# One decoder layer on one core: value banks emptied bank by bank, a pair's queries and keys projected one step ahead, the last product of the stick-breaking weights on VectorE

## The chip, the core and the metric

The kernel runs on one core of a Trainium2 chip. It is one launch, and the metric is the device time of that launch in microseconds. The engines that matter are TensorE (PE: matrix products, written into the eight banks of PSUM), VectorE (DVE), ScalarE (ACT), GpSimd (POOL) and the queue of SyncE (SP), which issues the loads of the weights.

## What is computed

One post-norm decoder layer over 512 positions of width 1024, batch 1:

```python
u = x * (1.0 + sc1) + sh1                       # adaLN, from c @ w_ada + b_ada
proj = u @ w_in                                 # q,k,v of both branches, forget logits, two gates
y_fox = forgetting_attention(q_a, k_a, v_a)     # 8 heads of 64: softmax(q k / 8 + c_t - c_s), causal
y_sb  = stick_breaking_attention(q_b, k_b, v_b) # 8 heads: beta[t,s] * prod_(s<j<t) (1 - beta[t,j])
merged = sigmoid(g_a) * (y_fox @ w_fox_proj) + sigmoid(g_b) * (y_sb @ w_sb_proj)
x = layer_norm(alpha * x + (1 + gt1) * (merged @ w_o))
u2 = x * (1.0 + sc2) + sh2
h_gate, h_val = split(causal_depthwise_conv(u2 @ w_up))
x = layer_norm(alpha * x + (1 + gt2) * ((silu(h_gate) * h_val) @ w_down))
```

In the stick-breaking branch beta is sigmoid(q k / 8). The product over the later keys is a running product of 1 - beta from the right; the weight is beta times that product.

## The kernel before

**Stages.** First comes an accumulation over the eight input tiles into all eight PSUM banks (lines 261 to 274): queries of pair 0 and 1, keys of pair 0, the values of the stick-breaking branch for the four blocks of 128 positions (banks `grp[3]` to `grp[6]`), and the forget logits. Then come sixteen heads of attention, eight stick-breaking and eight forgetting, in pairs (lines 727 to 762). Behind them come the branch projections, the output projection with the first norm, the up-projection and the down-projection.

**Every large product is made of three** (`mm3`, line 109): a float32 operand is split into a high part, written by ScalarE (`hi_of`, line 75), and a low part, written by VectorE (`lo_of`, line 78, input minus high part). A bank of PSUM that is emptied this way is read by ScalarE first and by VectorE after it, and an eight-bank pool (`bank`, line 66) hands the bank on when both have read it.

**A head** has three stages on TensorE. `stage_a` (line 411) makes the scores into three banks, four blocks of query positions in all; the one with 512 keys has the bank b == 1 to itself. For a stick-breaking head ScalarE then writes 1 - beta (`om`, line 452) and beta (`pt`, line 453) of each bank, VectorE scans `om` (line 456, four scans of 127, 383, 255 and 511 keys), and GpSimd multiplies `pt` by the scanned `om` (line 457, four products of the same sizes). `stage_b` (line 467) transposes the weights into three banks, which ScalarE and VectorE split into `ph`/`pl` and `ptc`. `stage_c` (line 490) multiplies by the values (`vv`).

**Fillers.** Projections that later heads and stages need stand in a list, `stream`: per pair the queries and the keys, then gates, value projections of the other branch and branch projections. A projection is a generator that gives three products at a time. `fill(n)` (line 710) takes n products from the list; `fill_to(mark)` (line 723) takes products until the list has passed a mark. `marks[(p, "k")]` is the place behind the keys of pair p. These fillers stand between the stages of the heads, so that TensorE has work while the other engines turn scores into weights. In the loop over the heads (lines 743 to 761) step n makes `stage_a` of head n + 2, `stage_b` of head n + 1 and `stage_c` of head n, with fillers between; `fill_to` for the pair of head n + 2 stands right ahead of that `stage_a`.

**What sets the order.** The order on SyncE is that of the code. On the other engines a scheduler sets it when the program is built, from the order of the code, the dependencies and the buffers that are free; the engines then run their instructions strictly in that order. So a change of the code can move instructions that it does not name.

## Time and profile before

| | us |
|---|---|
| runs before | 772.07, 772.87, 773.32 (median 772.87) |
| profiled execution, its own time | 772.12 |
| profiled execution, span of the core | 770.3 |
| TensorE busy in the span | 748.1 |
| VectorE busy | 549.4 |
| ScalarE busy | 350.4 |
| GpSimd busy | 185.7 |

The profile is one execution. Times in it run from the start of the span; 1.8 us of the execution's time lie outside of it. A row of the timeline gives the start, the duration, the engine, the line, the operation, what it writes and reads, how many like it follow each other, and in brackets how long the engine stood idle ahead of it and what ended that. Names of buffers are without their numbers there. Durations of instructions that follow each other overlap, so the distance from start to start is what an instruction costs in a row of them.

### The profile page before, as it was taken

How to read it: one execution, taken by the hardware profiler on the slowest of the kernel's cores; microseconds unless marked ns; L12 is line 12 of the kernel's file. 1: busy time of each engine (PE TensorE's matmuls, PEld its weight loads, DVE VectorE, ACT ScalarE, POOL GpSimd, SP SyncE). 2: the span in 40 equal slices, each digit the busy share in tenths (PEclk: the TensorE clock that was granted, in tenths of full speed). 3: DMA queues.
4: the chain of work that ended last, by engine and by line, in shares of the span. 5: the costliest groups of instructions: out<-in, count | busy, mean ns of one | idle time of the engine just before them, and what ended most of it. 6: DMA issues, size and time to landing. Idle time of an engine off the chain costs nothing.

```text
span 770.3 us, 9560 instructions
## 1 busy us (share of the span) xinstructions
PE 748.1 (97%) x3556; PEld 620.6 (81%) x3556; DVE 549.4 (71%) x822; ACT 350.4 (45%) x583; POOL 185.7 (24%) x138
## 2 busy tenths in 40 slices
PE   5998999999999999999999999999999999999995
PEld 3886887788888888888889888888888888888885
DVE  6979889966687977776676787686656665533666
ACT  3357686717667556333145434444444433222400
POOL 1025424510000011364000780000000043945500
PEclk9999999999999999999999999999999999999998
DMA  8951253542333323455302524354332214323202
GB/s 310 403 204 55 83 165 131 175 161 83 110 110 110 127 93 136 144 190 164 137 1 73 201 79 145 118 177 137 114 105 93 100 55 165 120 98 127 65 28 83
DMA packets 31105, 99.68 MB, mean 129 GB/s; under 512 B 4273, under 2 KB 4785, under 8 KB 31058
## 3 DMA queue, kind: packets, MB, share of 16 engines
q1 hardware_dynamic: 30546, 99.00, 37.0%
q8 instruction: 28, 0.46, 0.2%
q14 instruction: 19, 0.16, 0.1%
q0 software_dynamic: 512, 0.07, 0.1%
HBM read 96.88 MB, written 2.10 MB: 128 GB/s over the span
## 4 chain that ended last, share of the span: by engine, by line
PE 86%; DVE 6%; ACT 5%; DMA 1%; issue 1%; SPq 0%; DVEq 0%; ACTq 0%
PE ps L110 17%; PE ps L111 17%; PE ps L112 17%; PE ps L941 5%; PE ps L940 5%; PE ps L942 5%; PE ps L254 4%; PE ps L495 2%; PE ps L821 2%; PE ps L820 2%; PE ps L819 2%; PE ps L477 2%; DVE om L456 1%; DMA wa<-in_wa 1%; ACT wh L75 1%
## 5 line engine op out<-in xcount | busy, mean ns | idle before, releaser
L78 DVE TENSOR_TENSOR wl<-raw,wh 128x1024 fp32r<-128x1024 f32 (+2 forms) x106 | 143.8, 1357 | 101.0 <-ACT wh L75 100.5
L75 ACT ACTIVATE wh<-raw 128x1024 fp32r<-128x1024 f32 (+2 forms) x106 | 110.4, 1042 | 108.1 <-PE ps L942 39.9
L110 PE MATMUL ps<-u2h,wh 128*128 128x512 f32 (+1 forms) x376 | 141.4, 376 | 0.0
L111 PE MATMUL ps<-u2l,wh 128*128 128x512 f32 (+1 forms) x376 | 141.2, 376 | 0.0
L112 PE MATMUL ps<-u2h,wl 128*128 128x512 f32 (+1 forms) x376 | 141.2, 375 | 0.0
L587 POOL TENSOR_TENSOR raw<-raw,gt 128x1024 f32<-128x1024 f32 x22 | 60.7, 2774 | 187.1 <-DVE gt L550 157.6
L110 PE MATMUL ps<-uh,wh 128*128 128x512 f32 x232 | 92.9, 400 | 2.2 <-DVE vv L78 2.2
L112 PE MATMUL ps<-uh,wl 128*128 128x512 f32 x232 | 90.8, 391 | 0.0
L111 PE MATMUL ps<-ul,wh 128*128 128x512 f32 x232 | 90.8, 391 | 0.0
L110 PEld LDWEIGHTS ps<-u2h,wh 128*128 128x128 f32 x376 | 70.8, 188 | 12.9
L111 PEld LDWEIGHTS ps<-u2l,wh 128*128 128x128 f32 x376 | 70.8, 188 | 12.8
L112 PEld LDWEIGHTS ps<-u2h,wl 128*128 128x128 f32 x376 | 70.8, 188 | 12.6
L110 PEld LDWEIGHTS ps<-uh,wh 128*128 128x128 f32 x232 | 43.6, 188 | 10.7 <-DVE vv L78 2.5
L112 PEld LDWEIGHTS ps<-uh,wl 128*128 128x128 f32 x232 | 43.6, 188 | 9.4
L111 PEld LDWEIGHTS ps<-ul,wh 128*128 128x128 f32 x232 | 43.7, 188 | 7.9
L940 PE MATMUL ps<-wh,hh 128*128 128x512 f32 x128 | 49.8, 389 | 0.0
L941 PE MATMUL ps<-wl,hh 128*128 128x512 f32 x128 | 49.8, 389 | 0.0
L942 PE MATMUL ps<-wh,hl 128*128 128x512 f32 x128 | 49.8, 389 | 0.0
L457 POOL TENSOR_TENSOR pt<-pt,om 128x127 f32<-128x127 f32 (+3 forms) x32 | 40.0, 1278 | 33.8 <-DVE om L456 28.7
L75 ACT ACTIVATE hh<-cv 128x512 fp32r<-128x512 f32 x22 | 13.9, 631 | 59.6 <-DVE cv L920 59.6
L575 POOL TENSOR_TENSOR raw<-raw,gt 128x1024 f32<-128x1024 f32 x8 | 21.1, 2645 | 78.0 <-DVE m L78 42.2
L919 ACT ACTIVATE cv<-cv 128x512 f32<-128x512 f32 x22 | 13.9, 632 | 54.5 <-DVE cv L914 54.5
(188 smaller groups left out, 1463.0 us busy)
## 6 DMA issues: line engine op xcount, KB each, us to landing
raw<-in_wup SPq DMA_DIRECT2D x44, 512.0 KB, 3.3
raw<-in_wa SPq DMA_DIRECT2D x32, 512.0 KB, 3.3
raw<-in_wct SPq DMA_DIRECT2D x29, 512.0 KB, 3.2
raw<-in_wdn SPq DMA_DIRECT2D x22, 512.0 KB, 3.2
wa<-in_wa SPq DMA_DIRECT2D x14, 512.0 KB, 8.7
raw<-in_wp SPq DMA_DIRECT2D x8, 512.0 KB, 3.3
raw<-in_wo SPq DMA_DIRECT2D x8, 512.0 KB, 3.6
raw<-in_w SPq DMA_DIRECT2D x7, 452.0 KB, 8.3
```

What stands on the lines that cost most here:

```text
L75: S.activation(o, i, AF.Copy, scale=scale)
L78: return V.tensor_tensor(o, i, fl(hi), ALU.subtract)
L110: PE.matmul(ps, wh, ah, start=first, stop=False)
L111: PE.matmul(ps, wh, al, start=False, stop=False)
L112: PE.matmul(ps, wl, ah, start=False, stop=last)
L254: PE.matmul(grp[g], w, u, start=j == 0 and n == 0, stop=j == KT - 1 and n == (1 if g == 7 else 2))
L457: G.tensor_tensor(pt[b][:, s : e - 1], pt[b][:, s : e - 1], om[:, s + 1 : e], ALU.mult)
L575: G.tensor_tensor(r, r, gt[0], ALU.mult)
L587: G.tensor_tensor(r, r, gt[1], ALU.mult)
L940: PE.matmul(ps, hh[j][:, tb], w[0], start=first, stop=False)
L941: PE.matmul(ps, hh[j][:, tb], w[1], start=False, stop=False)
L942: PE.matmul(ps, hl[j][:, tb], w[0], start=False, stop=last)
```

## The change

It has three parts. The four value banks are emptied bank by bank (both halves of a bank, then the next bank) where they were emptied half by half (the first half of all banks, then the second). The fourth product of a stick-breaking head, that of bank b == 1 with 511 keys, goes from GpSimd to VectorE. And `fill_to` for a pair's keys moves: for pairs 2, 3, 4, 6 and 7 it now stands ahead of `stage_c` of the step before, where it stood ahead of `stage_a`; for pairs 1 and 5 it stays.

```diff
--- before.py
+++ after.py
@@ -454,7 +454,7 @@
                 for s, e in SEG[b]:
                     d0 = om[:, s + 1 : e][:, ::-1]
                     V.tensor_tensor_scan(d0, d0, zer.broadcast_to([P, e - s - 1]), 1.0, ALU.mult, ALU.add)
-                    G.tensor_tensor(pt[b][:, s : e - 1], pt[b][:, s : e - 1], om[:, s + 1 : e], ALU.mult)
+                    (V if b == 1 else G).tensor_tensor(pt[b][:, s : e - 1], pt[b][:, s : e - 1], om[:, s + 1 : e], ALU.mult)
         d["pt"] = pt
         scored.add(idx(br, h))
         if br == 0 and h + 4 < NH:
@@ -731,10 +731,11 @@
     q_evac(1, 1, grp[2])
     fill(6)
     stage_a(1, 0)
-    for half in range(2):
-        for j in range(NB):
+    for j in range(NB):
+        for half in range(2):
             v_evac(1, j, half, grp[3 + j])
-        fill(6)
+        if j % 2 == 1:
+            fill(6)
     stage_a(1, 1)
     fill(12)
     stage_b(1, 0)
@@ -745,7 +746,7 @@
             forget(last)
         f1, f2, f3 = FILL[n // 8]
         if n + 2 < 16:
-            if n % 2 == 0:
+            if n in (0, 8):
                 fill_to(marks[(n // 2 + 1, "k")])
             last = hd[heads[n + 1]].get("last")
             stage_a(*heads[n + 2])
@@ -753,6 +754,8 @@
         if n + 1 < 16:
             stage_b(*heads[n + 1])
         fill(f2)
+        if n % 2 == 1 and n != 7 and n + 3 < 16:
+            fill_to(marks[((n + 3) // 2, "k")])
         stage_c(b, h)
         if n == 7:
             lim[0] = marks["y0"]
```

What becomes of it on the engines is told by the order of the built program. Three places are shown, before and after.

**VectorE at the value banks.** `om_100` and `pt_96` belong to bank b == 1 of the first head; `vv_101` to `vv_108` are the eight halves of the value banks `ps_4` to `ps_7`; `wl_123` is the low half of a weight tile for a filler. Before:

```order
L78 TENSOR_TENSOR vv_101_617<-ps_4_106,vv_101_617 128x2x128
L78 TENSOR_TENSOR vv_102_620<-ps_5_107,vv_102_620 128x2x128
L78 TENSOR_TENSOR vv_103_623<-ps_6_108,vv_103_623 128x2x128
L78 TENSOR_TENSOR vv_104_626<-ps_7_109,vv_104_626 128x2x128
L78 TENSOR_TENSOR vv_105_635<-ps_4_106,vv_105_635 128x2x128
L78 TENSOR_TENSOR vv_106_638<-ps_5_107,vv_106_638 128x2x128
L78 TENSOR_TENSOR wl_123_706<-raw_85_562,wh_122_705 128x1024
L78 TENSOR_TENSOR vv_107_641<-ps_6_108,vv_107_641 128x2x128
L78 TENSOR_TENSOR vv_108_644<-ps_7_109,vv_108_644 128x2x128
```

After:

```order
L457 TENSOR_TENSOR pt_96_598<-pt_96_598,om_100_612 128x511
L78 TENSOR_TENSOR vv_101_617<-ps_4_106,vv_101_617 128x2x128
L78 TENSOR_TENSOR wl_123_706<-raw_85_562,wh_122_705 128x1024
L78 TENSOR_TENSOR vv_102_620<-ps_4_106,vv_102_620 128x2x128
L78 TENSOR_TENSOR vv_103_623<-ps_5_107,vv_103_623 128x2x128
L78 TENSOR_TENSOR vv_104_626<-ps_5_107,vv_104_626 128x2x128
L78 TENSOR_TENSOR vv_105_635<-ps_6_108,vv_105_635 128x2x128
L78 TENSOR_TENSOR vv_106_638<-ps_6_108,vv_106_638 128x2x128
L78 TENSOR_TENSOR vv_107_641<-ps_7_109,vv_107_641 128x2x128
L78 TENSOR_TENSOR vv_108_644<-ps_7_109,vv_108_644 128x2x128
```

The product stands ahead of all eight halves; the weight tile `wl_123` has moved from behind the sixth half to behind the first one; and the two halves of bank `ps_4` are now the first and the third row of their kind, where they were the first and the fifth. Further on in the same queue another weight tile, `wl_151`, has moved from behind the transposed weights of the second head to ahead of the second half of the keys of pair 1 (`m2_3`).

**TensorE at the third head.** `ps_120` is the bank of the filler (a gate), `ps_132` the last bank of the third head's scores, `ps_140`, `ps_143` and `ps_146` those of the second head's transposes, `ps_148` the bank of the next filler. Before:

```order
L425 MATMUL ps_132_739<-mskb_96,identb_88 128x128
L110 MATMUL ps_120_702<-uh_59_374,wh_88_568 128x512
L111 MATMUL ps_120_702<-ul_60_375,wh_88_568 128x512
L112 MATMUL ps_120_702<-uh_59_374,wl_89_569 128x512
L110 MATMUL ps_120_702<-uh_67_420,wh_88_568 128x512
L111 MATMUL ps_120_702<-ul_68_421,wh_88_568 128x512
L112 MATMUL ps_120_702<-uh_67_420,wl_89_569 128x512
L477 MATMUL ps_140_788<-ident_77,pt_112_668 128x128
L477 MATMUL ps_140_788<-ident_77,pt_114_670 128x128
L477 MATMUL ps_140_788<-ident_77,pt_112_668 128x128
L477 MATMUL ps_140_788<-ident_77,pt_113_669 128x128
L477 MATMUL ps_143_797<-ident_77,pt_114_670 128x128
```

After:

```order
L425 MATMUL ps_132_739<-mskb_96,identb_88 128x128
L477 MATMUL ps_140_788<-ident_77,pt_112_668 128x128
L477 MATMUL ps_140_788<-ident_77,pt_114_670 128x128
L477 MATMUL ps_140_788<-ident_77,pt_112_668 128x128
L477 MATMUL ps_140_788<-ident_77,pt_113_669 128x128
L477 MATMUL ps_143_797<-ident_77,pt_114_670 128x128
L477 MATMUL ps_143_797<-ident_77,pt_112_668 128x128
L477 MATMUL ps_143_797<-ident_77,pt_113_669 128x128
L477 MATMUL ps_146_805<-ident_77,pt_113_669 128x128
L477 MATMUL ps_146_805<-ident_77,pt_112_668 128x128
L477 MATMUL ps_146_805<-ident_77,pt_113_669 128x128
L110 MATMUL ps_148_816<-uh_19_149,wh_90_572 128x512
```

Before, the scores of the third head stood in the middle of the filler `ps_120`, and six of its products lay between them and the transposes. After, the whole filler stands ahead of the scores (some of it between the three groups of transposes of the first head), and scores, transposes of the second head and the next filler follow each other directly.

**TensorE at the first forgetting head.** `ps_340` before and `ps_336` after are the same bank by use: the keys of pair 4. `ps_354` holds that head's scores. `ps_350` before and `ps_346` after are the next filler. Before:

```order
L112 MATMUL ps_340_1733<-uh_71_458,wl_337_1698 128x512
L110 MATMUL ps_350_1782<-uh_19_149,wh_343_1740 128x512
L111 MATMUL ps_350_1782<-ul_20_150,wh_343_1740 128x512
L112 MATMUL ps_350_1782<-uh_19_149,wl_344_1741 128x512
L110 MATMUL ps_350_1782<-uh_27_190,wh_343_1740 128x512
L111 MATMUL ps_350_1782<-ul_28_191,wh_343_1740 128x512
L112 MATMUL ps_350_1782<-uh_27_190,wl_344_1741 128x512
L110 MATMUL ps_350_1782<-uh_35_236,wh_343_1740 128x512
L111 MATMUL ps_350_1782<-ul_36_237,wh_343_1740 128x512
L112 MATMUL ps_350_1782<-uh_35_236,wl_344_1741 128x512
L420 MATMUL ps_354_1794<-m1_345_1768,s1_338_1725 128x256
```

After:

```order
L112 MATMUL ps_336_1717<-uh_71_458,wl_333_1682 128x512
L110 MATMUL ps_346_1766<-uh_19_149,wh_339_1724 128x512
L111 MATMUL ps_346_1766<-ul_20_150,wh_339_1724 128x512
L112 MATMUL ps_346_1766<-uh_19_149,wl_340_1725 128x512
L495 MATMUL ps_350_1778<-ph_288_1429,vv_102_620 128x512
L495 MATMUL ps_350_1778<-ph_291_1437,vv_104_626 128x384
L495 MATMUL ps_350_1778<-ptc10_504,vv_106_638 128x256
L495 MATMUL ps_350_1778<-ptc10_504,vv_108_644 128x256
L495 MATMUL ps_350_1778<-pl_289_1430,vv_102_620 128x512
L495 MATMUL ps_350_1778<-pl_292_1438,vv_104_626 128x384
L495 MATMUL ps_350_1778<-ptc11_505,vv_106_638 128x256
L495 MATMUL ps_350_1778<-ptc11_505,vv_108_644 128x256
```

Before, nine products of the filler stand between the last one of the keys and the first scores that read them. After, three of them, the eight products of `stage_c` of the sixth head and another fifteen of the filler stand there. The first heads of pairs 6 and 7 are changed alike: nine before; after, fifteen and a `stage_c`. At pairs 2 and 3 the keys already stood well ahead of the scores that read them, and the order of TensorE there is the same before and after, apart from buffer numbers and two fillers that move within the transposes of the sixth head. ScalarE's program has two more loads of its function table (16 for 14), which the scheduler placed among the forgetting heads.

## Prediction

> **What bounds the kernel now.** I read the page first: its busy shares and its chain.
>
> ```profile
> PE 748.1 (97%) x3556; PEld 620.6 (81%) x3556; DVE 549.4 (71%) x822; ACT 350.4 (45%) x583; POOL 185.7 (24%) x138
> PE 86%; DVE 6%; ACT 5%; DMA 1%; issue 1%; SPq 0%; DVEq 0%; ACTq 0%
> ```
>
> TensorE is busy for 97% of the span and carries 86% of the chain that ended last. The change neither adds nor removes a product of TensorE, so all that it can move are the times in which TensorE waits. The waits of TensorE, summed by who ended them, come next; those in the attention stage are these:
>
> ```profile
> PE ps L110 <- DVE vv L78: 2.2, 1, 2.2
> PE ps L421 <- DVE m L78: 1.8, 2, 1.1
> PE ps L477 <- DVE yf L502: 1.0, 1, 1.0
> PE ps L420 <- ACT m L75: 0.4, 2, 0.2
> ```
>
> VectorE ends nearly all of them. The windows of the timeline say why: in one such stretch VectorE has 23.4 of 25 us filled.
>
> ```profile
> 120.00:145.00 25.00, 23.11 (x117) 18.59 (x115) 23.42 (x31) 17.84 (x33) 12.27 (x15) 1.00 0.37 128
> ```
>
> The fourth column group is VectorE's. So the question is what the change does to VectorE's queue at the few places where TensorE waits for it. Behind the attention stage TensorE has no wait that the change touches; what is won or lost ahead of 310 us stays to the end.
>
> **The change, part by part: the value banks and the product of the first three heads.** The rows around the two largest waits, from the timelines of VectorE, ScalarE and TensorE:
>
> ```profile
> 64.42 2.08 DVE L78 TENSOR_TENSOR vv<-ps,vv 128x256 fp32r<-128x256 f32 x6
> 66.58 1.23 DVE L78 TENSOR_TENSOR wl<-raw,wh 128x1024 fp32r<-128x1024 f32 x1
> 67.72 0.75 DVE L78 TENSOR_TENSOR vv<-ps,vv 128x256 fp32r<-128x256 f32 x2
> 68.38 3.75 DVE L456 TENSOR_TENSOR_SCAN om<-om,zer 128x127 f32<-128x127 f32 x4
> 72.05 0.65 DVE L78 TENSOR_TENSOR m<-ps,m 64x512 fp32r<-64x512 f32 x1
> 73.97 0.69 DVE L78 TENSOR_TENSOR m<-ps,m 64x512 fp32r<-64x512 f32 x1 [0.80 <-ACT m L75]
> 74.70 1.16 DVE L78 TENSOR_TENSOR pl<-ps,ph 128x512 fp32r<-128x512 f32 x2
> ```
>
> ```profile
> 64.88 0.71 ACT L75 ACTIVATE vv<-ps 128x256 fp32r<-128x256 f32 x2 [0.92 <-DVE vv L78]
> 72.74 1.20 ACT L75 ACTIVATE m<-ps 64x512 fp32r<-64x512 f32 x2 [1.60 <-DVE m L78]
> ```
>
> ```profile
> 66.23 0.50 PE L110 MATMUL ps<-uh,wh 128*128 128x512 f32 x1 [2.22 <-DVE vv L78]
> 72.76 0.38 PE L421 MATMUL ps<-m,s 68*128 68x256 f32 x1 [1.11 <-DVE m L78]
> 73.97 0.48 PE L110 MATMUL ps<-uh,wh 128*128 128x512 f32 x1
> 77.24 0.39 PE L110 MATMUL ps<-uh,wh 128*128 128x512 f32 x1
> ```
>
> At 66.23 TensorE starts a filler in the bank whose fifth half VectorE has just read (six halves from 64.42, 0.33 apart, 0.42 each: the fifth ends at 66.16). At 72.76 it goes on with the third head's scores once the low keys (`m`, ended 72.70) are there. At 77.24 the next filler begins; this row is my yardstick, since the same work lies ahead of it before and after.
>
> What a product of 511 keys costs on VectorE the trace does not show. The nearest rows are two-input operations of 512 columns:
>
> ```profile
> 92.81 1.06 DVE L529 SCALAR_TENSOR_TENSOR ac<-raw,cTs,ac 128x512 f32<-128x512 f32 x1
> 95.43 0.74 DVE L529 SCALAR_TENSOR_TENSOR ac<-raw,cTs,ac 128x512 f32<-128x512 f32 x1
> 142.83 1.58 DVE L78 TENSOR_TENSOR wvl<-raw,wvh 128x512 fp32r<-128x512 f32 x1
> 144.80 0.68 DVE L78 TENSOR_TENSOR wvl<-raw,wvh 128x512 fp32r<-128x512 f32 x1
> 121.98 1.27 DVE L78 TENSOR_TENSOR chi<-fq,chi 8x512 fp32r<-8x512 f32 x1
> ```
>
> In a row, 144.80 costs 0.60 to the next start, which is the lower end. But the same operation took 1.06 at 92.81, right behind the last scan, against 0.74 at 95.43, and another took 1.58 against 0.68: there GpSimd was still at its products. The moved product stands in the place of the row at 92.81, with GpSimd's product of 255 keys still running, so I take 0.60 + 0.32 = 0.92 where it follows the scan directly, and 0.60 where another operation has taken that delay already. [...]
>
> Now VectorE's queue as the built order has it. The product takes 64.42 to 65.34. The first half follows at 65.34, the weight tile at 65.67; that tile costs 1.14 (66.58 to 67.72), so the second half of the first bank starts at 66.81 and ends at 67.23: the filler starts at 67.3 where it started at 66.23, 1.1 later, although its bank is third in place of fifth. The other banks now go one after the other, and within a bank the two engines take turns: ScalarE's row at 64.88 shows that the second half of a bank waits until VectorE has read the first. A bank then costs 0.42 (VectorE), 0.39 (ScalarE; two take 0.71), 0.33 to VectorE's next start, and about 0.05 of hand-over: 1.19, where eight halves in a row cost 0.33 each. The first half of the second bank starts at 67.14, that of the fourth at 69.52, and its second half ends at 70.8. The second head's scans start there, where they started at 68.38: 2.4 later. [...]
>
> From the scans to the keys VectorE took 68.38 to 72.70, 4.32. From 70.8, with another product of 0.92, that is 76.05; TensorE has its fillers done by about 74 (24 of them from 67.3, and the first head's transposes) and waits for it. The rest of the scores takes 1.21 (72.76 to 73.97) and ends at 77.3. Now the transposes follow without six fillers between. All eight banks hold something then (keys, gate, three of transposes, three of scores), so each group needs a bank that VectorE has just let go, and the filler behind them the last one. VectorE: the third bank of transposes to 76.5, the weight tile that was moved here to 77.7 (1.14 again); the second keys, for which ScalarE takes 1.20 from 76.05, to 78.35; the two `pl` 1.16, to 79.5. The yardstick row comes at 79.5 in place of 77.24: **2.3 later**. With products at 0.60 it is 1.6; with ScalarE's sigmoid 0.2 late at the second scan it is 2.5.
>
> Is this caught up? VectorE and ScalarE go on from TensorE:
>
> ```profile
> 84.03 1.06 ACT L75 ACTIVATE wh<-raw 128x1024 fp32r<-128x1024 f32 x1 [1.97 <-PE ps L111]
> 85.13 1.22 DVE L78 TENSOR_TENSOR wl<-raw,wh 128x1024 fp32r<-128x1024 f32 x1 [2.28 <-ACT wh L75]
> 100.89 0.63 ACT L75 ACTIVATE yh<-yf 128x512 fp32r<-128x512 f32 x1 [1.14 <-DVE yf L502]
> 128.75 0.38 PE L421 MATMUL ps<-m,s 68*128 68x256 f32 x1 [0.68 <-DVE m L78]
> 144.93 0.50 PE L420 MATMUL ps<-m,s 128*128 128x512 f32 x1 [0.26 <-DVE ptc L78]
> ```
>
> At 85.13 VectorE has been idle for 2.28 until a weight tile that ScalarE could split only when TensorE had used its buffer. That idle time takes in the third head's product, and from there everything shifts with TensorE. So I count no catching up.
>
> **The products of heads four to eight.** From 85.13 VectorE has no gap until it releases ScalarE at 100.89; the fourth head's product (0.60, behind the row at 92.81) comes through to there, and on through ScalarE to the sixth head's scans. The sixth head's product adds 0.92 and takes away the slow `chi` at 121.98 (1.27 against some 0.68). At 128.75 TensorE waits for VectorE, so it is later by 0.60 + 0.92 - 0.59 = 0.93 less what the new order gains by placing a weight tile of ScalarE's (1.06, as at 84.03) into a gap; half of that, 0.5, gives +0.4 (0 to 0.9). At 144.93 the seventh head's product (0.60) replaces GpSimd's, for which the row at 142.83 had waited 0.90: -0.3. Sum **+0.1** (-0.5 to +0.8).
>
> **The keys one step ahead.** Three times TensorE reached scores whose keys ScalarE had not written yet. Here are two of them (181.22 and 245.39), and between them the same kind of scores without a wait (193.42):
>
> ```profile
> 180.66 0.39 PE L112 MATMUL ps<-uh,wl 128*128 128x512 f32 x1
> 181.22 0.74 PE L420 MATMUL ps<-m,s 128*128 128x256 f32 x3 [0.18 <-ACT m L75]
> 181.80 0.39 PE L110 MATMUL ps<-uh,wh 128*128 128x512 f32 x1
> 182.48 0.28 PE L421 MATMUL ps<-m,s 68*128 68x256 f32 x1
> 183.58 0.48 PE L110 MATMUL ps<-uh,wh 128*128 128x512 f32 x1
> 193.42 0.28 PE L420 MATMUL ps<-m,s 128*128 128x256 f32 x1
> 195.01 0.48 PE L110 MATMUL ps<-uh,wh 128*128 128x512 f32 x1
> 244.90 0.39 PE L112 MATMUL ps<-yh,wl 128*128 128x512 f32 x1
> 245.39 0.73 PE L420 MATMUL ps<-m,s 128*128 128x256 f32 x3
> ```
>
> A filler lasts 0.23 from start to start, so scores could have begun at 180.89: 0.33 lost. In two pieces they took 0.58 + 1.10 = 1.68 against 1.59 in one (193.42 to 195.01): 0.09 more. At 245.39 it is 0.26 + 0.09, and I take the same for the third (pair 7). Fifteen fillers and a `stage_c` hide the splitting afterwards (nine did not), so all three go: **-1.1** (-1.2 to -0.8). At pair 5 nothing changes. What is late next: `stage_c` of the waiting head comes after the keys, its inputs long done. The price at the end, where the list of fillers runs out earlier and the last head's transposes meet its `stage_c` with only the other head's eight products between, I put at nothing (0 to 0.5), and the two table loads of ScalarE too.
>
> **The sum.** 772.12 + 2.3 + 0.1 - 1.1 = 773.4 in the profiled execution. That execution lies 0.75 under the median of 772.87, so against the median I say 774.2, 0.17% more. A measurement of this kernel can tell about 0.2% from no change, 1.5 us, so this is no change by a narrow margin; the forecast's own range, from the ends above, is 773.0 to 775.4.
>
> **Rivals.** *VectorE becomes the bound from 85 to 145 us (slower).* The five later products would cost 0.92 each, with neither `chi` nor the row at 142.83 any quicker. At 128.75 three count, 2.8; at 144.93 the fourth, 0.9. For it: 23.42 of 25 us busy. Against it: GpSimd's slowing goes with its product. It gives 2.3 + 3.7 - 1.1 = +4.9, 777.8; it decides from two products at full price on. *The delay is swallowed (faster, or nearly).* If VectorE's chain to 145 does not hang on TensorE, the 2.3 only fill TensorE's waits there (1.8 and 1.0 in the first list, in part). Then -1.1 remain, and with 0.3 from each of two unslowed `ac` about -1.7: 771.2. Against it stands the row at 84.03. *The change does nothing that counts*: early products at 0.60, +1.6 - 0.5 - 1.1 = 0: 772.9.
>
> **Chances.** Forecast 0.6, of which 0.35 under +0.2% and 0.25 over it; VectorE bound 0.17; swallowed 0.13, of which 0.12 faster; nothing 0.10. So slower 0.42, same 0.46, faster 0.12. The range from 771.5 to 776.5 leaves out the far half of both outer rivals.
>
> **What would show it.** Right: a first filler about 1 us later than 66.23, scans of the second head at 70 to 71, the row of 77.24 at 79 to 80, no ScalarE wait at the first scores of pairs 4, 6 and 7, and the product on VectorE at 0.9 to 1.1 behind a scan. Wrong: the yardstick row near 77, or waits of TensorE between 85 and 145 that together grow by more than 1 us or vanish.

## The result and the profile after

The changed kernel takes 777.58 us (median of 4 runs, 777.02 to 778.18) against 773.1 us before (4 runs, 772.07 to 773.42): ratio 1.0062, 95% interval 1.0049 to 1.0074. The forecast was 774.2, with 776.5 as the upper end. The profiled execution took 777.68 (span 775.9), 5.56 more than that of before, of which the forecast had 1.3.

The busy shares and the chain, from the page of after:

```profile
PE 752.1 (97%) x3556; PEld 624.7 (81%) x3556; DVE 557.5 (72%) x830; ACT 353.9 (46%) x585; POOL 174.2 (22%) x130
...
PE 88%; DVE 5%; ACT 4%; issue 1%; DMA 1%; SPq 0%; DVEq 0%; ACTq 0%
```

TensorE is busy for 4.0 us more, although it makes the same 3556 products; why is told below. VectorE has the eight products (830 for 822). The waits of TensorE in after, summed by who ended them; what before had stands at the start of the prediction:

```profile
PE ps L110 <- DVE vv L78: 3.3, 1, 3.3
...
PE ps L421 <- DVE m L78: 1.6, 1, 1.6
PE ps L111 <- DVE yl L78: 1.0, 1, 1.0
PE ps L477 <- DVE m L78: 0.9, 1, 0.9
PE ps L420 <- ACT m L75: 0.5, 1, 0.5
```

The wait for `vv` grew by 1.1, as forecast. The wait for `yl`, the low part of an input of the branch projections, is new, and it lies where nothing was forecast. To see how much each place cost, the start of a product of TensorE is compared with the start of the same product before, at places ahead of which the same products lie in both:

```
at (us of before)    60.1   66.2   77.2  128.7  144.9  276    320    end
later in after      +0.07  +1.16  +3.94  +5.04  +4.86  +3.73  +5.47  +5.53
added since the last       +1.09  +2.78  +1.10  -0.18  -1.13  +1.74  +0.06
```

Less the 0.07 that was there at the start: +3.87 up to the yardstick row (forecast +2.3), +0.92 over heads four to eight (+0.1), -1.13 for the keys (-1.1), +1.74 at the end of attention (0 to 0.5). VectorE around the value banks in after:

```profile
64.54 0.87 DVE L457 TENSOR_TENSOR pt<-pt,om 128x511 f32<-128x511 f32 x1
65.45 0.42 DVE L78 TENSOR_TENSOR vv<-ps,vv 128x256 fp32r<-128x256 f32 x1
65.79 1.22 DVE L78 TENSOR_TENSOR wl<-raw,wh 128x1024 fp32r<-128x1024 f32 x1
66.92 0.75 DVE L78 TENSOR_TENSOR vv<-ps,vv 128x256 fp32r<-128x256 f32 x2
68.12 0.76 DVE L78 TENSOR_TENSOR vv<-ps,vv 128x256 fp32r<-128x256 f32 x2 [0.45 <-ACT vv L75]
...
71.02 3.75 DVE L456 TENSOR_TENSOR_SCAN om<-om,zer 128x127 f32<-128x127 f32 x4
74.87 0.88 DVE L457 TENSOR_TENSOR pt<-pt,om 128x511 f32<-128x511 f32 x1
75.67 0.67 DVE L78 TENSOR_TENSOR m<-ps,m 64x512 fp32r<-64x512 f32 x1
...
77.99 1.23 DVE L78 TENSOR_TENSOR wl<-raw,wh 128x1024 fp32r<-128x1024 f32 x1 [1.19 <-ACT wh L75]
79.25 0.69 DVE L78 TENSOR_TENSOR m<-ps,m 64x512 fp32r<-64x512 f32 x1
```

Down to 75.67 this is the forecast queue: the product at 0.87 and 0.88 (forecast 0.92), a bank in 1.20 from start to start (66.92 to 68.12; forecast 1.19), the scans at 71.02 (70.8), the low keys done at 76.34 (76.05). Then comes what was not forecast: VectorE stands still for 1.19 ahead of the weight tile at 77.99, because ScalarE's half of the tile is late, and ScalarE waited for a product of TensorE. ScalarE's row and then TensorE's:

```profile
76.90 1.06 ACT L75 ACTIVATE wh<-raw 128x1024 fp32r<-128x1024 f32 x1 [1.86 <-PE ps L111]
```

```profile
67.39 0.80 PE L110 MATMUL ps<-uh,wh 128*128 128x512 f32 x1 [3.34 <-DVE vv L78]
67.98 0.63 PE L111 MATMUL ps<-ul,wh 128*128 128x512 f32 x1
...
75.04 0.40 PE L111 MATMUL ps<-ul,wh 128*128 128x512 f32 x1
...
79.99 0.55 PE L477 MATMUL ps<-ident,pt 128*128 128x128 f32 x3 [0.91 <-DVE m L78]
...
81.18 0.50 PE L110 MATMUL ps<-uh,wh 128*128 128x512 f32 x1
```

The same product of 512 columns lasts 0.63 behind the wait and 0.40 later. Set out by windows of 3.41 us (the seventh number of a row, ahead of the DMA share, is the granted clock of TensorE), after shows:

```profile
63.04:66.46 3.42, 1.01 (x5) 0.42 (x4) 3.29 (x4) 1.75 (x4) 1.83 (x2) 1.00 0.00 0
66.46:69.87 3.41, 2.48 (x6) 2.00 (x7) 2.51 (x7) 1.42 (x5) 0.00 (x0) 0.50 0.44 154
69.87:73.29 3.42, 3.42 (x13) 2.76 (x12) 2.91 (x6) 3.18 (x8) 1.71 (x2) 0.50 0.00 0
...
131.32:134.74 3.42, 1.78 (x12) 1.36 (x11) 2.38 (x5) 0.93 (x3) 1.40 (x3) 1.00 0.82 280
134.74:138.15 3.41, 3.41 (x13) 2.41 (x12) 3.06 (x6) 2.54 (x5) 1.04 (x2) 0.50 0.03 10
```

After a window in which TensorE had work for only 1.01 of 3.42 us, the clock was granted at 0.50 for two windows; after one with 1.78, for one. Before, the window around the same wait had more work, and the clock stayed:

```profile
64.91:68.33 3.42, 2.10 (x12) 1.76 (x13) 3.35 (x8) 3.42 (x9) 0.96 (x1) 1.00 0.00 0
```

In after the half clock lasts 6.83 us from 66.46 and 3.41 from 134.74, and these two starts are 68.28 apart, 20 times 3.41. The windows of before lie some 1.9 later (64.91 for 63.04), though the program is only 0.07 apart at 60 us: where they lie against the program differs between these two executions.

That counts beside the length of the wait. In the profiled execution of the kernel with the keys alone (below), whose wait at this place is 2.24, where before had 2.22 and its window 2.10 us of work, a window happened to hold only 1.73 us of work, and the clock fell to 0.50 from 66.30 to 69.71. It cost nothing at the yardstick row (+0.00): the wait for the low keys, 1.11 before, took it up. In after the two windows were more than that wait could take up, and TensorE came to the third head's scores after the low keys.

At the end of attention, the rows of VectorE, GpSimd and TensorE in after, each in its own timeline:

```profile
311.80 1.97 DVE L78 TENSOR_TENSOR yl<-yf,yh 128x512 fp32r<-128x512 f32 x1 [0.70 <-ACT yh L75]
```

```profile
310.83 2.39 POOL L575 TENSOR_TENSOR raw<-raw,gt 128x1024 f32<-128x1024 f32 x1 [14.19 <-DMA raw<-in_wo]
```

```profile
313.83 0.49 PE L111 MATMUL ps<-yl,wh 128*128 128x512 f32 x1 [1.04 <-DVE yl L78]
```

And before:

```profile
307.18 0.69 DVE L78 TENSOR_TENSOR yl<-yf,yh 128x512 fp32r<-128x512 f32 x1 [0.70 <-ACT yh L75]
```

```profile
308.84 2.50 POOL L575 TENSOR_TENSOR raw<-raw,gt 128x1024 f32<-128x1024 f32 x1 [12.76 <-DMA raw<-in_wo]
```

Before, `yl` took 0.69 and was done at 307.87, before GpSimd began the product on the output weights. After, GpSimd began first, and `yl` took 1.97 and ended 0.55 behind GpSimd's end (313.77 against 313.22). TensorE, which has few fillers left there, waits for it. This meeting is the step of 1.28 in TensorE's delay between 307 and 310 us of before. Another 0.35 of the 1.74 is at the place that the prediction had named: the last head's `stage_c` comes so close behind its transposes that it waits for ScalarE's `ph` (two products take 0.93 in place of 0.58).

### The profile page after: what moved, and what is told of

Same layout as the page of the kernel before. It is cut to its first block, busy times and chain, and to the rows that moved or that the text cites. A ratio compares the mean times of both kernels' runs of the same rounds, so it can differ in the third digit from the quotient of the medians.

```text
span 775.9 us, 9551 instructions
## 1 busy us (share of the span) xinstructions
PE 752.1 (97%) x3556; PEld 624.7 (81%) x3556; DVE 557.5 (72%) x830; ACT 353.9 (46%) x585; POOL 174.2 (22%) x130
## 4 chain that ended last, share of the span: by engine, by line
PE 88%; DVE 5%; ACT 4%; issue 1%; DMA 1%; SPq 0%; DVEq 0%; ACTq 0%
PE ps L110 17%; PE ps L111 17%; PE ps L112 17%; PE ps L254 6%; PE ps L944 5%; PE ps L945 5%; PE ps L943 5%; PE ps L824 2%; PE ps L822 2%; PE ps L823 2%; PE ps L495 2%; PE ps L477 2%; ACT wh L75 1%; DVE wl L78 1%; PE ps L420 1%
## 5 line engine op out<-in xcount | busy, mean ns | idle before, releaser
L110 PE MATMUL ps<-uh,wh 128*128 128x512 f32 x232 | 94.5, 407 | 3.3 <-DVE vv L78 3.3
L112 PEld LDWEIGHTS ps<-u2h,wl 128*128 128x128 f32 x376 | 70.8, 188 | 12.9
L111 PEld LDWEIGHTS ps<-u2l,wh 128*128 128x128 f32 x376 | 70.8, 188 | 12.8
L110 PEld LDWEIGHTS ps<-u2h,wh 128*128 128x128 f32 x376 | 70.8, 188 | 12.6
L457 POOL TENSOR_TENSOR pt<-pt,om 128x127 f32<-128x127 f32 (+2 forms) x24 | 29.0, 1234 | 41.3 <-DVE om L456 31.6
```

Source lines behind the costliest of these rows:

```text
L110: PE.matmul(ps, wh, ah, start=first, stop=False)
L111: PE.matmul(ps, wh, al, start=False, stop=False)
L112: PE.matmul(ps, wl, ah, start=False, stop=last)
L457: (V if b == 1 else G).tensor_tensor(pt[b][:, s : e - 1], pt[b][:, s : e - 1], om[:, s + 1 : e], ALU.mult)
```

## The experiments

Two questions were open. For the attention stage: **Theory A** says that a good part of the delay is the slower clock that follows TensorE's longer waits; its rival, **Theory B**, says that VectorE's queue alone makes it, whatever the clock. For the end: **Theory A** says that `yl` is caught behind GpSimd's product; the rival is that the fillers taken forward are simply missing there. The table gives, for each kernel, how much later TensorE is than before at five places, less what it was at 60 us (from one profiled execution each). The times with the experiments are medians; the kernel before stood at 772.79, 773.13, 772.96, 773.02 and 773.08 beside them.

| kernel | at 60 | 77.2 | 128.7 | 144.9 | 276 | 320 |
|---|---|---|---|---|---|---|
| changed | +0.07 | +3.87 | +4.97 | +4.79 | +3.66 | +5.40 |
| the same again | +0.26 | +3.72 | +4.86 | +4.70 | +3.59 | +7.79 |
| value banks alone | +0.62 | +1.79 | +1.96 | +1.95 | +1.94 | +1.94 |
| product alone | -0.01 | +2.21 | +3.20 | +2.90 | +2.88 | +2.88 |
| keys alone | +0.63 | 0.00 | 0.00 | -0.01 | -1.10 | +0.70 |
| changed, first wait filled | +0.34 | +2.63 | +4.31 | +4.19 | +3.02 | +4.70 |
| changed, waits at 64 and 132 us filled | +1.58 | +2.75 | +4.28 | +4.92 | +4.04 | +6.22 |
| product alone, wait filled | +0.15 | +3.29 | +4.74 | +6.08 | +6.52 | +6.92 |
| product of heads 4 to 8 alone | +0.09 | -0.02 | +0.94 | +0.64 | +0.67 | +0.70 |

**The first wait filled.** Zero products behind the projection ahead of the wait keep TensorE at work; they add zeros to its sum.

```diff
+            if k == KT - 1 and more:      # keys of pair 1 only
+                for i in range(9):
+                    PE.matmul(ps, ptc[0][0][:, 0:128], uh[0], start=False, stop=i == 8)
```

> The changed kernel with nine more products of TensorE of a zero tile (128 columns by 512, 0.227 us each from start to start), added to the keys of pair 1 right before TensorE's long wait at 64 us; they add exact zeros, and all other instructions stand in the order of the changed kernel. TensorE then idles about 1.5 us before the filler at 67.4 in place of 3.6. Theory A (the slow stretch of TensorE from 66.5 to 73.3 us, granted clock 0.50, is what made 4.0 us out of the 2.3 us forecast for this stage): the clock stays at 1.0 there, the filler still starts at 67.4, the yardstick row (first filler behind the transposes of the second head) comes at 79.5 in place of 81.2, and the time is 775.9, 1.7 below the changed kernel's 777.6. Theory B (VectorE's queue alone makes the 4.0 us): the products change nothing, yardstick row at 81.2, time 777.6.

Measured: 778.14 (777.14 to 779.18, 5 runs), ratio 1.0069 (1.0056 to 1.0081). The windows and then TensorE's rows (lines of that kernel: 413 holds the zero products, 427 the scores):

```profile
66.60:70.00 3.40, 2.31 (x12) 1.96 (x13) 2.50 (x7) 1.58 (x5) 0.00 (x0) 1.00 0.50 153
...
130.58:133.99 3.41, 1.41 (x8) 0.80 (x7) 2.73 (x5) 0.93 (x2) 1.75 (x4) 1.00 0.86 272
133.99:137.41 3.42, 3.42 (x13) 2.61 (x12) 2.71 (x5) 2.89 (x6) 1.04 (x2) 0.50 0.11 41
```

```profile
64.19 2.22 PE L413 MATMUL ps<-uh,ptc 128*128 128x512 f32 x9
...
76.70 0.38 PE L427 MATMUL ps<-m,s 68*128 68x256 f32 x1 [1.57 <-DVE m L78]
...
133.40 0.38 PE L427 MATMUL ps<-m,s 68*128 68x256 f32 x1 [2.00 <-DVE m L78]
```

The clock stayed at 1.00 early, and the yardstick row came 1.24 sooner (+2.63 for +3.87). The weight tile that had come at 77.99 now followed VectorE's queue without a wait:

```profile
77.04 1.20 DVE L78 TENSOR_TENSOR wl<-raw,wh 128x1024 fp32r<-128x1024 f32 x1
```

So 1.24 is what the slow clock cost in this stage of the profiled execution. But the gain did not last: VectorE was no quicker, TensorE waited longer at 133.40, and by 144.9 only 0.60 of it was left. For the stage Theory A holds, for the time it fell.

**The parts alone.** The hunks of the diff, one by one.

> The kernel before with the first part alone (value banks emptied bank by bank). VectorE reads the first half of the first bank at 64.4, then the weight tile, so the first filler starts at 66.3 as before; a bank then costs 1.2 in place of 0.66, and the second head's scans start at 70.0 in place of 68.4. Theory A: +1.2 to +1.6 at the yardstick row, 774.5, and 1.7 more where TensorE's idle time falls so that its clock drops. Theory B (my prediction's rival that TensorE takes this up further on): under +0.3, 773.2.

> The kernel before with the second part alone (last product on VectorE). Theory A: the product stands ahead of the value halves, so the first filler starts 0.9 later (67.1) and TensorE idles 3.3 us; its clock drops as in the changed kernel. +0.9 in that stage from the queue and up to 1.7 from the clock, +0.7 from 85 to 150 us: 774.7 without and 776.4 with the slow clock. Theory B (VectorE bound from 85 to 145 us): the larger part, over 2 us, is added between 85 and 145.

> The kernel before with the third part alone (fill_to ahead of stage_c). Theory A (read from the trace after: the waits at pairs 4, 6 and 7 go, but the fillers taken forward are missing at the end of the forgetting heads, where the branch projection waits for the last head): -1.0 us up to 290 us, then +1.7 between 290 and 315, so +0.7 in sum, 773.8. Theory B (the end is late only because the other two parts shifted what runs beside it): -1.1, 772.0.

Measured: value banks 774.85 (11 runs), 1.0025 (1.0016 to 1.0034); product 775.23 (5 runs), 1.0032 (1.0020 to 1.0045); keys 773.64 (11 runs), 1.0011 (1.0002 to 1.0020). Over the 772.79 beside them these are +2.06, +2.44 and +0.85, together 5.35, where the whole change gave 4.5 to 5.5. These prices hold the clock as well: all three profiled executions have half-clock windows near 67 us (67.61 to 71.02, 66.22 to 73.04 and 66.30 to 69.71). Two parts cost, and the third, forecast at -1.1, costs as well: it wins 1.10 up to 276 and loses 1.80 behind it. Its `yl` shows the same meeting as in after, VectorE first and then GpSimd:

```profile
307.60 2.05 DVE L78 TENSOR_TENSOR yl<-yf,yh 128x512 fp32r<-128x512 f32 x1 [0.70 <-ACT yh L75]
```

```profile
306.70 2.40 POOL L575 TENSOR_TENSOR raw<-raw,gt 128x1024 f32<-128x1024 f32 x1 [14.30 <-DMA raw<-in_wo]
```

`yl` starts 0.42 later than before here, GpSimd's product 2.14 sooner. That fits the fillers that are missing: what stands behind them in the list is reached sooner.

**The changed kernel again.** A second set of runs.

> The changed kernel once more, to stand beside the kernel with the nine added products on equal terms. Theory A (the slow clock early on costs 1.3 us at the yardstick row, of which some 0.7 is given back around 134 us): 777.6, and at most 0.7 above what the kernel with the added products shows over many runs. Theory B (the slow clock costs nothing that stays, VectorE's queue sets the end of the stage): no difference between the two.

Measured: 778.61 (777.17 to 780.58, 6 runs), 1.0069 (1.0056 to 1.0083). With the first four there are now ten runs, and each has its mean granted clock: four at 0.995 or 0.996 took 777.02 to 777.65, four at 0.991 or 0.992 took 777.68 to 779.04, two at 0.987 and 0.988 took 780.58 and 780.42. One half-clock window more is 0.5 x 3.41 / 776 = 0.0022 of the mean clock; from 0.9955 to 0.9875 that is some 3.6 windows for about 3.1 us, an estimate of 0.9 us for each, if the mean clock is all that sets these runs apart. The runs of before at 0.995 or 0.996 in these comparisons took 772.2 to 773.8 (medians 772.9 and 772.8). So at the same mean clock the changed kernel is still some 4.4 us later: the clock widens its scatter, but most of the median is VectorE's queue and the end.

The profiled execution of this set, the slowest of the ten, is like the first one up to 276 us (+3.59 for +3.66) and loses 4.20 at the end of attention in place of 1.74:

```profile
311.92 2.83 DVE L78 TENSOR_TENSOR yl<-yf,yh 128x512 fp32r<-128x512 f32 x1 [0.70 <-ACT yh L75]
```

```profile
311.84 2.36 POOL L575 TENSOR_TENSOR raw<-raw,gt 128x1024 f32<-128x1024 f32 x1 [14.65 <-DMA raw<-in_wo]
```

GpSimd's product, which waits for a load, began just ahead of `yl`, so `yl` lay behind all of it; TensorE waited 1.90 in place of 1.04, its clock fell to 0.50 from 315.51 to 318.92, and with no wait behind it that window cost about 1.6, an estimate (the 2.46 lost more, less the 0.86 of longer wait). So the price of the end differs from one execution to the next, and the clock can have a part in it.

**The product of the later heads alone.** On VectorE for heads four to eight, the rest as before:

```diff
-                    G.tensor_tensor(pt[b][:, s : e - 1], ...)
+                    (V if b == 1 and h > 2 else G).tensor_tensor(pt[b][:, s : e - 1], ...)
```

> The kernel before with the last product on VectorE for heads four to eight alone (GpSimd keeps that of the first three). My prediction gave +0.1 for these heads (772.9); the trace of the second part alone shows +0.97 at the wait for the low keys near 129 us, -0.5 near 135 and +0.15 near 145, so Theory A: +0.65, 773.4. Theory B (all of the second part's cost comes from the value banks): 0, 772.8.

Measured: 773.94 (11 runs), 1.0013 (1.0004 to 1.0021). TensorE at the seventh head's scores:

```profile
129.78 0.39 PE L421 MATMUL ps<-m,s 68*128 68x256 f32 x1 [1.63 <-DVE m L78]
```

The wait was 0.68 before and is 1.63: 0.95 more, the two products less the unslowed `chi` (0.67 for 1.27), in full. Of it 0.47 goes at the wait for `yf` at 135, which before had 1.0. At 144.9 there is 0.17 again. So +0.7, not +0.1, without any half-clock window in that stretch.

**Banks two at a time.** The first halves of two banks, then their second halves:

```diff
-    for j in range(NB):
+    for j in (0, 2):
         for half in range(2):
-            v_evac(1, j, half, grp[3 + j])
-        if j % 2 == 1:
-            fill(6)
+            for i in (j, j + 1):
+                v_evac(1, i, half, grp[3 + i])
+        fill(6)
```

> The kernel before with the value banks emptied two at a time (first halves of two banks, then their second halves, then the other two). Two banks let the two engines work side by side, so a half costs 0.33 as before. The weight tile moves to third place, so the first filler starts at 66.6 in place of 66.2, and the second head's scans still start at 68.4. Theory A (what costs 2 us in the first part is the taking of turns within one bank, and the first filler's start is worth nothing while the low keys end at 72.7): 0, 772.8. Theory B (a bank let go later is what costs): +0.4 or more, 773.2.

Measured: 774.75 (11 runs), 1.0019 (1.0009 to 1.0028), +0.98 at the yardstick row where banks one by one have +1.79. VectorE there:

```profile
66.02 1.85 DVE L78 TENSOR_TENSOR wl<-raw,wh 128x1024 fp32r<-128x1024 f32 x1
67.79 2.28 DVE L78 TENSOR_TENSOR vv<-ps,vv 128x256 fp32r<-128x256 f32 x6
```

The turns are gone: six halves in 2.28, on average 0.37 from one to the next (0.33 before). But the weight tile still stands ahead of them, and now it meets GpSimd's product (done at 65.87 before, so at about 66.79 here, 0.92 later) and takes 1.85 for 1.23. I had expected no change, and that was wrong. How much the turns cost is read from the start of the second head's scans, here and with the banks one by one:

```profile
70.14 3.75 DVE L456 TENSOR_TENSOR_SCAN om<-om,zer 128x127 f32<-128x127 f32 x4
```

```profile
70.63 3.75 DVE L456 TENSOR_TENSOR_SCAN om<-om,zer 128x127 f32<-128x127 f32 x4
```

Less the delay at 60 us (0.92 and 0.62) they start 0.84 and 1.63 later than before. With the banks one by one the tile costs 1.13 (1.14 before), so the 1.63 is the turns; in pairs 0.63 of the 0.84 is the tile that meets GpSimd. The +0.98 at the yardstick row is no clean price of VectorE's queue: TensorE ran at half the clock from 67.93 to 71.34 and reached the third head's scores at 75.48, 1.0 after the low keys were done.

**The taken products deducted.** Keys alone; the fill behind `stage_c` takes as many products fewer as were taken ahead of it.

```diff
-            fill_to(marks[((n + 3) // 2, "k")])
+            took = fill_to(marks[((n + 3) // 2, "k")])
...
-        fill(f3)
+        fill(f3 - took)
```

> The kernel before with the third part alone, but the products that fill_to takes ahead of stage_c are taken off the fill behind it, so that the list of fillers is as long at the end as before. Theory A (the 1.7 us at the end of the forgetting heads come from fillers that were used up): the waits at pairs 4, 6 and 7 go and nothing is paid at the end: -1.0, 771.8. Theory B (the end is paid for the two additional table loads of ScalarE or for another order there): +0.7, 773.5. If the nine fillers in between were what hid the keys' splitting, the waits at pairs 4, 6 and 7 come back: 772.8.

Measured: 774.06 (11 runs), 1.0013 (1.0004 to 1.0021). The end is now right (+0.37 from 296 to 320), but the waits for the keys are back and larger, in the list of TensorE's waits 1.5 in four where before had 0.4 in two:

```profile
PE ps L420 <- ACT m L75: 1.5, 4, 0.9
```

The expected gain is missing: what removed those waits were the additional fillers between keys and scores, and these are the fillers that the end lacks. Gain and price cannot be had apart in this way.

**The meeting at the end.** Keys alone, with the output-weight product in two halves on GpSimd, or on VectorE:

```diff
-        G.tensor_tensor(r, r, gt[0], ALU.mult)
+        for e in range(2):
+            c = slice(e * 512, (e + 1) * 512)
+            G.tensor_tensor(r[:, c], r[:, c], gt[0][:, c], ALU.mult)
```

```diff
-        G.tensor_tensor(r, r, gt[0], ALU.mult)
+        V.tensor_tensor(r, r, gt[0], ALU.mult)
```

> The third part alone, with GpSimd's product of a row of the output weights (1024 columns, 2.4 us) made in two halves; the order of all engines is that of the third part alone. There VectorE's yl of the last head took 2.05 us in place of 0.70 and ended 0.55 after GpSimd's product. Theory A (VectorE can't start on two SBUF inputs until the GpSimd instruction under way ends): yl starts its work when the first half ends, the wait of the branch projection falls from 1.28 to about 0.1, and the time from 773.6 to 772.5. Theory B (yl is late for want of fillers alone, or GpSimd's second half goes ahead of VectorE): the wait stays at 1.2 to 1.3, 773.6.

> The third part alone, with all eight products of the output weights on VectorE in place of GpSimd. Theory A: no instruction of GpSimd stands beside yl; yl takes 0.70, the wait of the branch projection is at most 0.3, and the time falls from 773.6 to about 772.5. Theory B (the used-up fillers alone): the wait stays over 1 us, 773.6 or more, since VectorE has eight products of 1.2 us more.

Measured: halves 773.48 (11 runs), 1.0004 (0.9996 to 1.0013); on VectorE 772.33 (11 runs), 0.9993 (0.9984 to 1.0002). VectorE with the halves, then with the whole product on VectorE:

```profile
307.90 1.59 DVE L78 TENSOR_TENSOR yl<-yf,yh 128x512 fp32r<-128x512 f32 x1 [0.70 <-ACT yh L75]
309.42 2.37 DVE L78 TENSOR_TENSOR wol<-raw,woh 128x512 fp32r<-128x512 f32 x2
```

```profile
307.48 1.22 DVE L575 TENSOR_TENSOR raw<-raw,gt 128x1024 f32<-128x1024 f32 x1
308.62 0.68 DVE L78 TENSOR_TENSOR yl<-yf,yh 128x512 fp32r<-128x512 f32 x1
```

Without GpSimd's product `yl` takes 0.68 again, TensorE has no wait there, and the kernel is 1.3 us quicker than keys alone, as Theory A says. Halves shorten `yl` only to 1.59 and pass the rest on to the next two operations (2.37 for two that take 1.28 otherwise); TensorE's wait fell from 1.11 to 0.66 only, not to the 0.1 that Theory A gave.

**Is it the move itself?** The kernel before with the output-weight product on VectorE; and keys alone with that and the keys of pair 5 ahead as well.

> The kernel before with the products of the output weights on VectorE and nothing else. TensorE has no wait that GpSimd's products cause there. Theory A (the 1.3 us that this move brought to the third part are the meeting with yl alone): no change, 772.9. Theory B (the move is a gain by itself): 771.6.

> The third part alone, for the keys of pair 5 too, with the products of the output weights on VectorE. With pairs 2, 3, 4, 6 and 7 this was 772.3. Theory A (a pair's keys one stage_c and fifteen fillers earlier take its wait away): the wait at pair 5, 0.6 there, goes too: 771.7, 0.15% under the kernel before. Theory B (the fillers it takes are missing at the end): 772.3 or more.

Measured: 772.96 (11 runs), 0.9997 (0.9988 to 1.0006), no change; and 772.36 (11 runs), 0.9991 (0.9982 to 1.0000). So the 1.3 is the meeting and not a cheaper product. Pair 5's wait is gone, and another of 0.21 has come at 221. These are the two quickest kernels of the study, 0.07% and 0.09% under before, at the edge of what can be told.

**The changed kernel without the meeting.** The same line on VectorE in the whole change.

> The changed kernel with the products of the output weights on VectorE. Theory A (the meeting of GpSimd's product with yl makes 1.3 us of the change's cost): the wait of the branch projection at 314 us falls under 0.3, the time by 1.3 from 777.6 to 778.6 down to 776.3 to 777.3. Theory B: no change.

Measured: 776.88 (775.95 to 777.82, 5 runs), 1.0046 (1.0033 to 1.0058): 0.7 to 1.7 us less than the changed kernel's two sets, and the wait for `yl` gone. In its profiled execution TensorE stood at +2.74 at the yardstick row with one half-clock window (68.70 to 72.11): a later wait for VectorE swallowed it.

**More waits filled.** The zero products with the product part alone; with the whole change at three waits; and at two, with narrower ones at the seventh head:

```diff
+            for _ in range({(1, 6, 0): 12}.get((br, h, i), 0)):     # in stage_a, behind the first product
+                PE.matmul(bk[b][:, o : o + w], ptc[0][0][:, 0:128], uh[0][:, 0:w], start=False, stop=False)
```

> The second part alone, with nine more products of a zero tile in TensorE's long wait at 64 us; the order of all engines is that of the second part alone. There TensorE's clock was 0.50 from 66.2 to 73.0 and the third head's scores found the low keys ready (they ended 73.96, 1.26 later than before), so TensorE and not VectorE set the stage's end. Theory A (the slow clock costs what VectorE does not): the delay at the yardstick row is 1.3 in place of 2.2, 774.3 in place of 775.2. Theory B: 2.2, 775.2.

> The changed kernel with products of a zero tile in all three long waits of TensorE: nine at 64 us, five at the third head's scores (75 us), eleven of 256 columns at the eighth head's scores (132 us); they add exact zeros. The order of VectorE and ScalarE is that of the changed kernel up to 150 us, with small differences behind. Theory A (the slow clock makes 1.3 us of the early stage and some 0.2 to 0.5 near 135, the rest is VectorE's queue): the clock stays at 1.0 throughout, the yardstick row at about 79.9, 776.0, and the times scatter less than the changed kernel's (777.0 to 780.6). Theory B (VectorE's queue makes all of it, TensorE only waits elsewhere): 777.6 or more.

> The changed kernel with nine products of a zero tile in TensorE's wait at 64 us and twelve of 256 columns in its wait at 132 us (seventh head); they add exact zeros. The order of VectorE and ScalarE is that of the changed kernel up to 150 us. Theory A (the queue of VectorE makes 2.7 us of the early stage and about 0.7 of the later heads, the slow clock the rest): clock 1.0 up to 150 us, delay there 3.4 to 3.8 over the kernel before where the changed kernel has 4.7. Theory B (VectorE's chain is as late without the slow clock): 4.4 to 4.7, as with the first filling alone.

Measured: 778.32 (6 runs), 1.0068 (1.0056 to 1.0080); 780.22 (5 runs), 1.0096 (1.0079 to 1.0113); 778.98 (5 runs), 1.0069 (1.0055 to 1.0083). None came near what its Theory A gave. In the first the wait moved to the next place, and the clock fell behind that one, where nothing swallows it; TensorE, then windows:

```profile
74.18 0.39 PE L427 MATMUL ps<-m,s 68*128 68x256 f32 x1 [1.96 <-DVE m L78]
```

```profile
72.20:75.59 3.39, 1.43 (x11) 1.21 (x11) 3.19 (x5) 1.39 (x3) 0.27 (x1) 1.00 0.51 155
75.59:79.00 3.41, 3.41 (x10) 2.56 (x9) 3.38 (x6) 3.29 (x8) 1.25 (x2) 0.50 0.00 0
```

In the second, the third filling fell on the head behind the intended one, where TensorE did not wait, and cost 1.3 itself; it tells nothing of the total. The third has the clock at 1.00 through the stretch from 128 to 145, and TensorE is as late there as in the changed kernel (+4.92 for +4.79); but it has a half-clock window from 79.09 to 82.50, so it does not decide alone. Three other kernels have no such window between the yardstick row and 145 us: product alone, product of heads four to eight alone, and the changed kernel without the meeting. They lose 0.69, 0.66 and 0.83 on this stretch, the changed kernel 0.92. That is Theory B for these heads: VectorE's chain is late, whatever the clock.

## Why the prediction was wrong

**The value banks and the first three heads: +2.3 forecast, +3.87 in the profiled execution.** The mechanism was right to within 0.3 down to the low keys at 76. The step that failed is "TensorE has its fillers done by about 74 ... and waits for it". They were done at 76.9, since two windows ran at half the clock, and so the weight tile that I had put at 76.5 came at 77.99. With the clock kept at 1.00 the stage cost 2.63 to 2.75: the queue itself was 0.3 to 0.45 larger than forecast. The trace of before had shown slow products behind an idle TensorE, its first ones, behind a wait of 6.18, which I overlooked:

```profile
10.29:13.70 3.41, 3.24 (x8) 2.57 (x9) 2.99 (x7) 1.80 (x5) 0.00 (x0) 1.00 1.00 327
13.70:17.11 3.41, 3.41 (x17) 2.77 (x15) 2.70 (x6) 0.59 (x1) 0.00 (x0) 1.00 1.02 410
```

The clock's column reads 1.00 in both (the trace holds a clock only from 13.70 on), but eight products take 3.24 in the first where 17 fit into the second: 0.43 and 0.23 from start to start. The prediction asked what a longer wait does to VectorE, and not what it does to TensorE; its first step, that the change can move nothing but the times in which TensorE waits, left out that the products themselves can take longer (TensorE busy 752.1 for 748.1 us). Nor was the half clock sure to come: with waits of 2.24 and 2.22 a window of keys alone held 1.73 of work and the clock fell, that of before held 2.10 and it stayed.

**Heads four to eight: +0.1 forecast, +0.92.** The step "half of that, 0.5" for a weight tile placed into a gap failed: it gained nothing, and the 0.95 arrived in full at 128.75. The -0.3 at 144.93 did not come either (+0.17 with the product of these heads alone). "VectorE becomes the bound" named the right mechanism at the wrong price: the +3.7 that it put there measured +0.7 to +0.9, so that its 777.8 lies near the result is chance.

**The keys: -1.1 forecast, -1.13.** The mechanism was right: the three waits went. The sum is right in part by luck: they gave 0.54, 0.45 and 0.45, more than forecast, and the wait at pair 5, where nothing was to change, grew from 0.20 to 0.46.

**The end: 0 (0 to 0.5) forecast, +1.74.** The step "the price at the end ... I put at nothing" failed, and in the first profiled execution it is the largest miss that the clock has no part in (in the second one the clock added to it). The list of fillers was said to run out earlier; the price of that was judged from the heads' own stages and not from what runs on the other engines there: the heads' own part measured 0.35, inside the range, the meeting of `yl` with GpSimd's product 1.28. The slowing of a VectorE operation beside GpSimd's products, read from rows of before (1.06 for 0.74 at 92.81, 1.58 for 0.68 at 142.83), was applied to the early products and not here, since before had the two operations one behind the other (`yl` done at 307.87, the product begun at 308.84). The experiment with deducted fillers shows besides that the -1.1 and this price come from the same fillers; with the output-weight product on VectorE 0.46 of the price is left (from 276 to 320 in that profiled execution).

**The sum.** By the starts of TensorE's products 3.87 + 0.92 - 1.13 + 1.74 = 5.40, where the forecast had 1.3. Against the medians the change is 4.5, since the profiled execution of before lies 1.0 under its median. Of the 3.2 that the medians differ from the forecast, the end has about 1.7 (by the first profiled execution), heads four to eight 0.6 to 0.8, the early queue 0.3 to 0.45. What is left, 0.3 to 0.6, fits the clock, which in a single execution cost 0 to 1.2 in the early stage, and the end, which cost 2.5 more in the second profiled execution; how much of a median each is stays open, because no experiment held the clock at 1.00 through a whole execution.

## What to carry to other kernels

Work that is taken forward as cover is missing where it was taken from: look at the end of the list as closely as at the place that gains, and at which operations of VectorE and GpSimd meet when it is reached at another time. A wait of TensorE cost more than its length here where it left a window of 3.41 us about half idle (1.01 and 1.78 us of work in after), and whether that showed depended on whether a later wait swallowed it (1.24 at the yardstick row in the changed kernel, 0.00 in keys alone). Filling waits with empty products bought nothing (778.14, 780.22 and 778.98 for 777.58 and 778.61; 778.32 for 775.23): the engine that was waited for was no quicker.

## What the runs showed of the hardware

- The granted clock of TensorE fell to 0.50 for windows of 3.41 us, in a kernel whose TensorE is busy for 97%. It fell behind the windows with 1.01 and 1.78 us of work in after (63.04 and 131.32), 1.41 with the first wait filled (130.58), 1.43 with the product alone and its wait filled (72.20) and 0.86 in the changed kernel without the meeting (65.28); it stayed behind 2.10 in before (64.91) and 2.31 with the first wait filled (66.60). In the product of the later heads the wait of 1.63 leaves 1.78 or more of such a window, and the products behind it last 0.39, as at the full clock. Out of the half clock, the window with 2.48 of work (66.46 in after) was followed by another at 0.50, those with 3.42 and 3.41 (69.87 and 134.74 in after) by 1.00; what decides there the traces do not show.
- The same kernel's runs scattered from 777.02 to 780.58, by and large in the order of their mean clock (0.996 to 0.987).
- `yl`, a VectorE operation of two SBUF inputs, takes 0.68 or 0.69 alone; it took 1.97, 2.05 and 2.83 beside a GpSimd product of 2.4, and ended 0.55 after it each time. Splitting GpSimd's product brought it to 1.59 and moved the waiting to the next two operations (2.37 for 1.28).
- Two halves of one bank that ScalarE and VectorE read in turns cost 1.20 a bank (66.92 to 68.12 in after); with two banks read alternately six halves took 2.28, 0.37 from one to the next, and half by half over all four banks, in before, 0.33.
